# A decoder block on one core: ScalarE alone reads the transposed FFN input, the first weight group has its own buffer, and its preparation is interleaved with the residual adds

## The chip, the cores and the metric

One Trainium2 chip, one of its cores. The metric is the device time of one execution in microseconds. Three runs of the kernel before took 842.82, 843.07 and 843.86; their median is 843.07. One further execution was taken by the hardware profiler, and the profile and the trace are of that one.

The engines have these names here: PE does matmuls (PEld its weight loads), DVE is VectorE, ACT is ScalarE, POOL is GpSimd, and SP issues DMAs. Each works through its own queue in program order, and they meet through semaphores.

## The reference, cut to what matters

One decoder layer over 512 positions and 1024 channels in fp32. What bears on this change is the end of the first sub-layer and the start of the second:

```python
    x = x + gate1 * (merged @ w_out)
    h2 = rms_norm(x, norm2_g) * (1.0 + scale2) + shift2
    f_g, f_u = jnp.split(h2 @ w_ffn_in, 2, axis=-1)
    x = x + gate2 * ((jax.nn.silu(f_g) * f_u) @ w_ffn_out)
```

Ahead of it stand adaLN modulation, a combined input projection, a gated MLP over chunks and a sparse attention with an indexer; behind it stands a final RMSNorm. D_FF is 2816.

## The kernel before, in words

The kernel is one program with an order written out by hand: each engine executes in the order in which the Python code names its instructions. Each fp32 matrix product is made of three matmuls (`mm3`, L51 to L55): every operand is split into a high part, a copy rounded to the matmul type that ACT makes, and a low part, the remainder, that DVE (sometimes POOL) makes by a subtraction; the products high × high, high × low and low × high are added in PSUM. So each block of weights costs one ACT and one DVE instruction before PE may use it.

Weights come through a stream. `ensure(i)` issues the DMAs of the coming entries as long as one of the three rotating `raw` buffers can be promised (L92), and does the split of all entries up to `i` (`prep`: ACT at L112, the low part at L116). An entry can name fixed buffers (`where`) in place of the rotating `hi` and `lo`, and can have its low part put off (`"later"`), which then is done by calling `stream[i]["do"]()`.

The stretch around the change has these stages:

- **The output projection's last products** (loop from L1341). PSUM tiles `po`: for each half of the positions (two tiles of 128 rows) and each half h of the columns, two weight entries `W_O` give 24 matmuls of 512 columns. `resid` (L1152) then does, for each of the two row tiles, a DVE multiply by the gate (L1155), a DVE add into x (L1156) and an ACT square with a sum along the row (L1157). Meanwhile `ensure` splits the four entries `WF0` of the first FFN weights.
- **The norm of a half.** `row_rstd` (L1159) reduces the sums on DVE and takes the power on POOL. `norm2_x` (L1172) scales one row tile on DVE (L1179) and one on ACT (L1177).
- **The transposition.** `norm2_T(half)` (L1181) makes four PSUM banks `x2T` of four transposes each (PE, L1198). Each bank holds two blocks of 128x256. In the kernel before, DVE reads one block with scale and shift (L1208) and ACT the other (L1206); ACT makes the high part of both (L1210) and DVE the low part (L1213). `norm2_T(0)` stands amid the last products of the second half, `norm2_T(1)` amid the first FFN matmuls.
- **The first FFN columns** (`pf`, L1554 on): 192 matmuls of 256 columns, first for half 0, then for half 1. `t_diff` (L1410) and `t_split` (L305, L306) make from the blocks of both halves the four sums and differences that the next stage needs.
- **The seven-product groups** (loop over q from −2 to 17, tiles `R`). Each is a Strassen-like scheme of seven products on 2x2 blocks of a weight group. `s_issue(q)` (L1232) loads the two raw tiles of a group, `s_prep(q)` gives four pairs of an ACT split and DVE work on them (a0, d0 at L1257 to L1262; a1, d1 at L1266 to L1270; a2, d2 at L1274 and L1277; a3, d3 at L1281 and L1284). The work for group q+1 is put between the products of group q.

For the first group, q = −2, that work stands ahead of the loop: the raw tiles take two of the three rotating `raw` buffers and are issued after the first residuals; a0 and d0 stand behind `norm2_x(0)`; a2, d2, a1 and d1 behind `norm2_x(1)`; a3 and d3 amid the `t_split` calls of half 1. The order between residuals, norm and block work is:

```python
            for e in range(2):
                resid(po[e], 512 * h, 512, h, 2 * half + e, gate_b[1])
            if half == 0:
                ensure(WF0[2 + h])
                if h == 0:
                    s_issue(-2)
        if half == 0:
            for e in range(2):
                row_rstd(e)
            norm2_x(0)
            pre = s_prep(-2)
            for fn in pre[0]:
                fn()
```

Of the kernel before, what the change touches and what calls it, by code (L numbers as in the profile page):

```python
# [28 lines left out]
def block_kernel(ctx: ExitStack, tc: tile.TileContext, x, positions, w_ada, b_ada, w_in,  # L29
# [15 lines left out]
    def f(ap):  # L45
        return ap.bitcast(F32)
# [208 lines left out]
    for g in range(4):  # L255
# [903 lines left out]
    def row_rstd(tk):  # L1159
        V.tensor_reduce(r2[:, tk:tk + 1], ss2[:, tk], op=OP.add, axis=AX.X)  # L1160
        P.tensor_tensor(r2[:, tk:tk + 1], r2[:, tk:tk + 1], mhalf[:, :1], op=OP.pow)  # L1161


    HB = {}
    for kh in range(2):
        for th in range(2):
            HB[kh, th] = [base.tile([128, 4, 256], F32R, name="h2", tag=f"S2_{(kh * 2 + th) * 2 + e}", bufs=1)
                          for e in range(2)]
    h2f = {}
    xn = {}  # L1170

# [9 lines left out]
    def norm2_T(half, also={}):  # L1181
        if half == 0:
            for kh in range(2):
                t = ffn[0].tile([128, 4, 256], F32, name="h2f", tag=f"F{kh}", bufs=1)
                h2f["t", kh, 0] = [t[:, 0:2], t[:, 2:4]]
        else:
            for kh in range(2):
                h2f["t", kh, 1] = []
                for q in range(2):
                    t = base.tile([128, 2, 256], F32, name="h2f", tag=f"S1_{kh * 2 + q}", bufs=1)  # L1190
                    h2f["t", kh, 1].append(t)
        low = []
        for k2 in range(4):
            p = bank(4 + k2, "x2T")
            for k in range(2):
                kt = k2 * 2 + k
                for e in range(2):
                    T.transpose(p[:, k * 256 + e * 128:k * 256 + (e + 1) * 128],  # L1198
                                xn[2 * half + e][:, kt * 128:(kt + 1) * 128], ident)
            hf = h2f["t", k2 // 2, half][k2 % 2]  # L1200
            for k in range(2):
                kt = k2 * 2 + k
                g, s = Gc[:, 1, kt:kt + 1], Gc[:, 1, 8 + kt:9 + kt]
                src = p[:, k * 256:(k + 1) * 256]
                if k:
                    A.activation(hf[:, k], src, AF.Identity, scale=g, bias=s)  # L1206
                else:
                    V.tensor_scalar(hf[:, k], src, g, s, op0=OP.mult, op1=OP.add)  # L1208
            hi, lo = (t[:, 2 * (k2 % 2):2 * (k2 % 2) + 2] for t in HB[k2 // 2, half])
            A.activation(hi, hf, AF.Copy)  # L1210
            while low:
                low.pop()()
            low.append(lambda a=lo, b=hf, c=hi: V.tensor_sub(a, b, f(c)))  # L1213
            for fn in also.get(k2, ()):
                fn()
        low.pop()()


    NQ = 18
# [2 lines left out]
    def s_issue(q):  # L1222
        if q >= NQ:
            return
        c0 = (2 + q // 2) * 256 + (DFF if q % 2 else 0)
        sraw[q] = []
        for kh in range(2):
            if q % 2 and kh:
                t = ffn[0].tile([128, 4, 2, 128], F32, name="raw", tag="F0" if q > 0 else "E5", bufs=1)
            else:  # L1230
                t = base.tile([128, 4, 2, 128], F32, name="raw", tag="raw", bufs=RAWB)
            SY.dma_start(t.rearrange("p j a n -> p j (a n)"),  # L1232
                         w_ffn_in[kh * 512:(kh + 1) * 512, c0:c0 + 256].rearrange("(j p) n -> p j n", p=128))
            sraw[q].append(t)
# [10 lines left out]
    def s_prep(q):  # L1245

        if q >= NQ:
            return z_first()
        ra, rb = sraw[q]
        d = sw[q] = {}  # L1250
        A11, A21, A12, A22 = ra[:, :, 0], ra[:, :, 1], rb[:, :, 0], rb[:, :, 1]

        def a0():
            d["A"] = tuple(base.tile([128, 4, 128], F32R, name="sa", tag="acc", bufs=2) if q == -2 else
                           base.tile([128, 4, 128], F32R, name="sa", tag=f"S1_{4 + 2 * (q % 2) + e}", bufs=1)
                           for e in range(2))
            A.activation(d["A"][0], A11, AF.Copy)  # L1257

        def d0():
            V.tensor_add(A21, A21, A22)  # L1260
            V.tensor_sub(d["A"][1], A11, f(d["A"][0]))
# [23 lines left out]
        return [(a0, d0), (a1, d1), (a2, d2), (a3, d3)]  # L1285


    def seed(Z, ZB, dst, src):
# [49 lines left out]
    ffn.append(ctx.enter_context(tc.tile_pool(name="ffn", bufs=1)))  # L1338
    ensure(W_O[3])
    add_kept(O, 3, 2)  # L1340
    for half in range(2):  # L1341
        for h in range(2):
            po = O[2 * half + h]
            for n_, i in enumerate(W_O[2 * h:2 * h + 2]):
                hi, lo = chunk[i]
                for e in range(2):
                    opt_a_mm(po[e], 2 * half + e, hi, lo, stream[i]["kts"], mT, 8, False)
                if (half, h, n_) == (0, 0, 0):
                    ensure(WF0[1])
                if (half, h, n_) == (1, 1, 0):  # L1350
                    norm2_T(0)
            for e in range(2):
                resid(po[e], 512 * h, 512, h, 2 * half + e, gate_b[1])
            if half == 0:
                ensure(WF0[2 + h])
                if h == 0:
                    s_issue(-2)
        if half == 0:
# [12 lines left out]

    gate_b[2] = base.tile([128, D], F32, name="gate2b", tag="gate", bufs=1)
# [34 lines left out]

    TB = {}

    def t_diff():  # L1410
        for q in range(2):
# [144 lines left out]
    for half in range(2):  # L1556
        o = slice(half * 256, (half + 1) * 256)
        for w in range(2):
            for ci, i in enumerate(W_F[w]):
                hi, lo = chunk[i]  # L1560
                for j, kt in enumerate(stream[i]["kts"]):
                    for m in range(2):
                        cc = slice(m * 128, (m + 1) * 128)
                        mm3(pf[w][m][:, o], (hi[:, j, cc], lo[:, j, cc]), tuple(t[:, j] for t in HB[ci, half]),
                            kt + half == 0, kt == 7, skip_group_check=True)
                if half == 0 and w == 1 and ci == 0:
                    norm2_T(1)
            if half == 0 and w == 1:
                t_diff()
            if half == 1 and w == 0:  # L1570
                s_issue(-1)
            if half == 1:
                if w == 0:
                    EV[w](0)(pf[w])
                t_split(w + 1)
                if w == 1:
                    for fn in pre[3]:
                        fn()
                    t_split(3)
                    EV[w](0)(pf[w])  # L1580
                    t_split(4)
# [8 lines left out]
    for q in range(-2, NQ):  # L1590
# [30 lines left out]
        pre[0][0]()  # L1621
        sprod(R[0], d["A"], HB[0, 0], True)
        A.activation(R[1], R[0], AF.Copy)  # L1623
        pre[0][1]()
# [6 lines left out]
        pre[1][0]()  # L1631
        pre[1][1]()
        sprod(R[1], S2_, TB[2], False)
        A.activation(R[2], R[1], AF.Copy)
        pre[2][0]()
# [235 lines left out]
```

## Time and profile before

| what | us |
|---|---|
| median of three runs | 843.07 |
| lowest and highest of them | 842.82, 843.86 |
| the profiled execution, by the clock of the device | 842.46 |
| its span, first to last instruction | 840.7 |

Its mean granted TensorE clock is 0.995 of full speed. The busy shares of the engines follow below with the lines that the prediction rests on.

A timeline row gives the start in microseconds from the start of the span, the duration, engine and line, the operation with the tile that it writes and those that it reads, and in brackets the idle time of the engine before it and the instruction that ended it. A row of waits gives what waited for what, the total, the count and the longest. A row of groups gives the count, then busy time and mean duration in ns, then the idle time before. A window row gives for each engine its busy time and its count of instructions, then the granted clock of PE (1.00 is full speed), the share of the DMA engines and the GB/s. A matmul's duration is longer than the distance to the next one, since they are pipelined; what a matmul costs is the distance from start to start.

### The profile page before, as it was taken

Reading aid. Unit: us, or ns where it says so; the run is one execution under the profiler, and the core shown is the slowest. Engines: PE = TensorE matmul, PEld = TensorE weight load, DVE = VectorE, ACT = ScalarE, POOL = GpSimd, SP = SyncE. Lnnn points to the kernel's source line nnn. Section 1 sums busy time; section 2 is a strip of 40 time slices with the busy share of each in tenths; the row PEclk is TensorE's granted clock in tenths of the full one; section 3 lists DMA queues with packets and bytes.
Section 4 is the critical chain, followed back from the end, with each engine's and each line's share of the span. In section 5 each row is a group of like instructions: output and inputs, shape, how many; then the busy total and the mean of one; then the engine's idle time right before and its main releaser. Section 6 shows DMA issues by size and latency. Waiting matters only on the chain. (4 is left out here: it accounts for less than half of the span.)

```text
span 840.7 us, 12867 instructions
## 1 busy us (share of the span) xinstructions
PE 824.4 (98%) x4980; PEld 733.6 (87%) x4980; DVE 678.3 (81%) x1169; ACT 410.1 (49%) x714; POOL 108.3 (13%) x101
## 2 busy tenths in 40 slices
PE   7999999999999999999999989999999999999996
PEld 6888889988888888988888879999999999888885
DVE  7978799788899558887697779889998888985635
ACT  5664445322332226665536457555555555663322
POOL 2060022353344411000000000000000000000001
PEclk9999999999999999999999999999999999999998
DMA  9962362432346652047532402345543334143212
GB/s 297 308 193 71 96 200 77 127 89 86 106 147 199 190 172 90 26 154 228 196 100 62 139 26 76 109 157 163 167 158 102 102 101 147 54 141 104 82 50 101
DMA packets 95677, 109.10 MB, mean 130 GB/s; under 512 B 5616, under 2 KB 76272, under 8 KB 95616
## 3 DMA queue, kind: packets, MB, share of 16 engines
q1 hardware_dynamic: 92512, 101.37, 39.6%
q0 software_dynamic: 2384, 6.10, 2.1%
q8 instruction: 39, 0.64, 0.3%
q10 hardware_dynamic: 720, 0.82, 0.3%
q14 instruction: 22, 0.18, 0.1%
HBM read 105.90 MB, written 2.10 MB: 128 GB/s over the span
## 5 line engine op out<-in xcount | busy, mean ns | idle before, releaser
L112 ACT ACTIVATE hi<-raw 128x1024 fp32r<-128x1024 f32 (+2 forms) x82 | 84.6, 1034 | 106.2 <-PE pb L54 35.3
L116 DVE TENSOR_TENSOR lo<-raw,hi 128x1024 fp32r<-128x1024 f32 (+2 forms) x46 | 55.5, 1211 | 43.3 <-ACT hi L112 43.2
L116 POOL TENSOR_TENSOR lo<-raw,hi 128x1024 fp32r<-128x1024 f32 x29 | 73.3, 2529 | 128.5 <-ACT hi L112 122.8
L53 PE MATMUL pb<-h,hi 128*128 128x512 f32 x192 | 76.4, 398 | 0.0
L55 PE MATMUL pb<-h,lo 128*128 128x512 f32 x192 | 75.8, 395 | 0.0
L54 PE MATMUL pb<-hl,hi 128*128 128x512 f32 x192 | 75.8, 395 | 0.0
L177 DVE SCALAR_TENSOR_TENSOR acc<-mraw,cols,acc 128x512 f32<-128x512 f32 x49 | 39.8, 812 | 17.9 <-DMA mraw<-in_w_ada_dram 16.8
L55 PE MATMUL pfo<-hi,gs 128*128 128x512 f32 (+1 forms) x126 | 46.5, 369 | 0.0
L54 PE MATMUL pfo<-lo,gs 128*128 128x512 f32 (+1 forms) x126 | 46.4, 369 | 0.0
L53 PE MATMUL pfo<-hi,gs 128*128 128x512 f32 (+1 forms) x126 | 46.4, 368 | 0.0
L53 PE MATMUL R<-tb,sx 128*128 128x256 f32 x160 | 45.3, 283 | 0.5 <-ACT R L1623 0.5
L54 PE MATMUL R<-tb,sx 128*128 128x256 f32 x160 | 45.1, 282 | 0.0
L55 PE MATMUL R<-tb,sx 128*128 128x256 f32 x160 | 45.1, 282 | 0.0
L53 PE MATMUL R<-tb,hi 128*128 128x256 f32 x160 | 44.9, 281 | 0.0
L55 PE MATMUL R<-tb,lo 128*128 128x256 f32 x160 | 44.8, 280 | 0.0
L54 PE MATMUL R<-tb,hi 128*128 128x256 f32 x160 | 44.6, 279 | 0.0
L55 PEld LDWEIGHTS pb<-h,lo 128*128 128x128 f32 x192 | 36.0, 188 | 8.8
L54 PEld LDWEIGHTS pb<-hl,hi 128*128 128x128 f32 x192 | 36.0, 188 | 8.3
L53 PEld LDWEIGHTS pb<-h,hi 128*128 128x128 f32 x192 | 36.0, 188 | 8.3
L54 PE MATMUL pav<-lo,h 128*128 128x256 f32 x128 | 35.8, 280 | 0.0
L53 PE MATMUL pav<-hi,h 128*128 128x256 f32 x128 | 35.8, 279 | 0.0
L55 PE MATMUL pav<-hi,hl 128*128 128x256 f32 x128 | 35.8, 279 | 0.0
(400 smaller groups left out, 2660.7 us busy)
## 6 DMA issues: line engine op xcount, KB each, us to landing
raw<-in_w_ffn_in_dram SPq DMA_DIRECT2D x44, 512.0 KB, 4.3
raw<-in_w_in_dram SPq DMA_DIRECT2D x40, 512.0 KB, 3.9
mraw<-in_w_ada_dram SPq DMA_DIRECT2D x28, 512.0 KB, 4.1
raw<-in_w_ffn_out_dram SPq DMA_DIRECT2D x17, 512.0 KB, 3.9
s<-in_w_ada_dram SPq DMA_DIRECT2D x30, 256.0 KB, 5.5
raw<-in_w_proj_a_dram SPq DMA_DIRECT2D x8, 512.0 KB, 4.8
raw<-in_w_proj_b_dram SPq DMA_DIRECT2D x8, 512.0 KB, 4.7
raw<-in_w_in_dram SPq DMA_DIRECT2D x9, 256.0 KB, 4.7
```

Source lines behind the costliest of these rows:

```text
L53: T.matmul(o, wh, rh, start=start, stop=False, **kw)
L54: T.matmul(o, wh, rlo, start=False, stop=False, **kw)
L55: T.matmul(o, wlo, rh, start=False, stop=stop, **kw)
L112: A.activation(hi[:, :m], e["raw"][:, :m], AF.Copy)
L116: e["lo"].tensor_sub(lo[:, :m], e["raw"][:, :m], f(hi[:, :m]))
L177: V.scalar_tensor_tensor(o, w, cs[:, j:j + 1], o, op0=OP.mult, op1=OP.add)
```

## The change

1. **ACT alone reads the transposed banks.** In `norm2_T` both blocks of a bank are read by ACT; the DVE read goes. The low parts are not done in `norm2_T` any more: it returns them as a list, and the caller places them.
2. **A buffer of their own for the raw blocks of group −2.** They go to a tile `E2` of the `ffn` pool, which later holds the first `t_split` result, in place of two rotating `raw` buffers; `s_issue(-2)` moves ahead, behind `ensure(WF0[1])`.
3. **The block work of group −2 is interleaved with the residuals.** d0 and d1 are cut in two (d0a, d0b, d1a, d1b), and all of a0 to a3 and d0 to d3 are done by the end of the output projection. The low parts of the third and fourth FFN entries are put off and placed by hand. The reduces of half 0 come ahead of them.
4. **Other places for the weights of the output projection.** All four `W_O` entries have fixed buffers among `S2_0` to `S2_7`, those of column half 0 in the ones that half 0 of the FFN input takes afterwards, those of column half 1 in the ones for half 1. Accordingly the tiles `HB` are allocated in `norm2_T`.
5. **`t_diff` is called for one part at a time** in half 1, the first part ahead of the last low part.

```diff
-           ((0, 4, ("S2_2", "S2_3")), (0, 6, ("S2_6", "S2_7")), (1, 4, None), (1, 6, None))]
+           ((0, 4, ("S2_0", "S2_1")), (0, 6, ("S2_4", "S2_5")), (1, 4, ("S2_2", "S2_3")), (1, 6, ("S2_6", "S2_7")))]
...
-                if k:
-                    A.activation(hf[:, k], src, AF.Identity, scale=g, bias=s)
-                else:
-                    V.tensor_scalar(hf[:, k], src, g, s, op0=OP.mult, op1=OP.add)
+                A.activation(hf[:, k], p[:, k * 256:(k + 1) * 256], AF.Identity, scale=Gc[:, 1, kt:kt + 1],
+                             bias=Gc[:, 1, 8 + kt:9 + kt])
             hi, lo = (t[:, 2 * (k2 % 2):2 * (k2 % 2) + 2] for t in HB[k2 // 2, half])
             A.activation(hi, hf, AF.Copy)
-            while low:
-                low.pop()()
             low.append(lambda a=lo, b=hf, c=hi: V.tensor_sub(a, b, f(c)))
-            for fn in also.get(k2, ()):
-                fn()
-        low.pop()()
+        return low
...
+        both = ffn[0].tile([128, 2, 4, 2, 128], F32, name="raw", tag="E2", bufs=1) if q == -2 else None
         for kh in range(2):
-            if q % 2 and kh:
+            if both is not None:
+                t = both[:, kh]
+            elif q % 2 and kh:
...
-        def d0():
+        def d0a():
             V.tensor_add(A21, A21, A22)
+
+        def d0b():
             V.tensor_sub(d["A"][1], A11, f(d["A"][0]))
             V.tensor_sub(A11, A21, A11)
...
-        def d1():
+        def d1a():
             V.tensor_sub(d["B"][1], rb, f(d["B"][0]))
+
+        def d1b():
             V.tensor_sub(rb, rb, A11[:, :, None, :].to_broadcast([128, 4, 2, 128]))
...
+    for w in WF0[2:4]:
+        stream[w]["lo"] = "later"
...
                 if (half, h, n_) == (0, 0, 0):
                     ensure(WF0[1])
+                    s_issue(-2)
                 if (half, h, n_) == (1, 1, 0):
-                    norm2_T(0)
-            for e in range(2):
-                resid(po[e], 512 * h, 512, h, 2 * half + e, gate_b[1])
-            if half == 0:
-                ensure(WF0[2 + h])
-                if h == 0:
-                    s_issue(-2)
-        if half == 0:
-            for e in range(2):
-                row_rstd(e)
-            norm2_x(0)
-            pre = s_prep(-2)
-            for fn in pre[0]:
-                fn()
-    for e in range(2, 4):
-        row_rstd(e)
-    norm2_x(1)
-    for fn in pre[2] + pre[1]:
-        fn()
+                    low = norm2_T(0)
+            if (half, h) == (0, 0):
+                res(0)
+                ensure(WF0[2])
+                res(1)
+                stream[WF0[2]]["do"]()
+                (a0, d0a, d0b), (a1, d1a, d1b), (a2, d2), (a3, d3) = s_prep(-2)
+                a0()
+            elif (half, h) == (0, 1):
+                res(0)
+                res(1)
+                ensure(WF0[3])
+                d0a()
+                row_rstd(0)
+                row_rstd(1)
+                norm2_x(0)
+                d0b()
+                a2()
+            elif (half, h) == (1, 0):
+                res(0)
+                res(1)
+                stream[WF0[3]]["do"]()
+                d2()
+                a1()
+            else:
+                low[0]()
+                d1a()
+                low[1]()
+                res(0)
+                low[2]()
+                low[3]()
+                res(1)
+                row_rstd(2)
+                row_rstd(3)
+                norm2_x(1)
+                d1b()
+                a3()
+                d3()
...
                 if half == 0 and w == 1 and ci == 0:
-                    norm2_T(1)
-            if half == 0 and w == 1:
-                t_diff()
+                    low = norm2_T(1)
+                    for fn in low[:3]:
+                        fn()
+                    t_diff(0)
+                    low[3]()
+                    t_diff(1)
...
                 if w == 1:
-                    for fn in pre[3]:
-                        fn()
                     t_split(3)
```

More of the change, by code (lines that the diff above doesn't have):

```diff
@@ L1164, in block_kernel @@
     HB = {}
[L1165 to L1168, printed above, removed]
     h2f = {}
@@ L1179, in norm2_x, with norm2_T @@
                 V.tensor_scalar(xn[tk], xt[tk], r2[:, tk:tk + 1], None, op0=OP.mult)
-    def norm2_T(half, also={}):
-        if half == 0:
-            for kh in range(2):
+    def norm2_T(half):
+        for kh in range(2):
+            HB[kh, half] = [base.tile([128, 4, 256], F32R, name="h2", tag=f"S2_{(kh * 2 + half) * 2 + e}", bufs=1)
+                            for e in range(2)]
+            if half == 0:
                 t = ffn[0].tile([128, 4, 256], F32, name="h2f", tag=f"F{kh}", bufs=1)
                 h2f["t", kh, 0] = [t[:, 0:2], t[:, 2:4]]
-        else:
[L1187 to L1191, printed above, removed]
+            else:
+                h2f["t", kh, 1] = [base.tile([128, 2, 256], F32, name="h2f", tag=f"S1_{kh * 2 + q}", bufs=1)
+                                   for q in range(2)]
         low = []
@@ L1284, in d3 @@
             V.tensor_sub(d["D"][1], rb, f(d["D"][0]))
-        return [(a0, d0), (a1, d1), (a2, d2), (a3, d3)]
+        return [(a0, d0a, d0b), (a1, d1a, d1b), (a2, d2), (a3, d3)]
     def seed(Z, ZB, dst, src):
@@ L1343, in block_kernel, with res @@
             po = O[2 * half + h]
+            def res(e):
+                resid(po[e], 512 * h, 512, h, 2 * half + e, gate_b[1])
             for n_, i in enumerate(W_O[2 * h:2 * h + 2]):
@@ L1408, in block_kernel, with t_diff @@
     TB = {}
-    def t_diff():
-        for q in range(2):
+    def t_diff(*qs):
+        for q in qs:
             b11, b21, b12, b22 = (h2f["t", kh, th][q] for th in range(2) for kh in range(2))
@@ L1623, in block_kernel @@
         A.activation(R[1], R[0], AF.Copy)
-        pre[0][1]()
+        for fn in pre[0][1:]:
+            fn()
         while left:
@@ L1630, in block_kernel @@
         A.activation(ps[0], R[3], AF.Copy)
-        pre[1][0]()
-        pre[1][1]()
+        for fn in pre[1]:
+            fn()
         sprod(R[1], S2_, TB[2], False)
```

5 lines of the change are left out of this document (1 added, 4 removed).

## The prediction

> **What bounds the kernel now.** I read the page first, then the waits of PE, then PE's own instructions in order of time.
>
> ```profile
> span 840.7 us, 12867 instructions
> PE 824.4 (98%) x4980; PEld 733.6 (87%) x4980; DVE 678.3 (81%) x1169; ACT 410.1 (49%) x714; POOL 108.3 (13%) x101
> raw<-in_w_ffn_in_dram SPq DMA_DIRECT2D x44, 512.0 KB, 4.3
> PE pf L53 <- ACT h L1210: 2.8, 2, 1.9
> ```
>
> PE is busy 98% of the span, so only what makes PE stand still or run slowly can give time. The row of waits (total, times, longest) ends on the transposed input of the FFN: its first matmuls (pf) wait for the high part of the block (ACT, L1210) and, in the next fence, for its low part (DVE, L1213). That is the place that the change touches. The next fence is PE in order of time around it: start, duration, line, and in brackets the idle time before.
>
> ```profile
> 484.55 0.39 PE L54 MATMUL po<-lo,mt 128*128 128x512 f32 x1
> 484.78 0.40 PE L55 MATMUL po<-hi,mt 128*128 128x512 f32 x1
> 487.09 0.39 PE L53 MATMUL pf<-h,wx 128*128 128x256 f32 x1 [1.91 <-ACT h L1210]
> 487.81 0.39 PE L54 MATMUL pf<-h,wx 128*128 128x256 f32 x1 [0.34 <-DVE h L1213]
> ...
> 491.56 0.30 PE L54 MATMUL pf<-h,wx 128*128 128x256 f32 x1
> ...
> 497.87 1.91 PE L1198 MATMUL x2T<-cst,xn 128*128 128x128 f32 x16
> 499.54 0.36 PE L53 MATMUL pf<-h,wx 128*128 128x256 f32 x1
> ...
> 502.35 0.28 PE L55 MATMUL pf<-h,wx 128*128 128x256 f32 x1
> 503.54 0.38 PE L53 MATMUL pf<-h,wx 128*128 128x256 f32 x1 [0.92 <-ACT h L1210]
> 504.26 0.39 PE L54 MATMUL pf<-h,wx 128*128 128x256 f32 x1 [0.34 <-DVE h L1213]
> ...
> 515.61 0.28 PE L53 MATMUL R<-h,sa 128*128 128x256 f32 x1
> ...
> 528.37 0.28 PE L55 MATMUL R<-tb,sx 128*128 128x256 f32 x1
> 529.11 0.39 PE L53 MATMUL R<-tb,sx 128*128 128x256 f32 x1 [0.46 <-ACT R L1623]
> ```
>
> And the same stretch in windows (PE busy and its count first, then the other engines, then the granted clock):
>
> ```profile
> 487.90:491.56 3.66, 3.66 (x19) 3.66 (x20) 3.06 (x6) 2.53 (x5) 0.00 (x0) 0.53 0.00 0
> 491.56:497.87 6.31, 6.31 (x54) 6.31 (x54) 3.23 (x7) 3.30 (x6) 2.07 (x3) 1.00 0.09 32
> ```
>
> At full clock a 256-column matmul comes every 6.31/53 = 0.119 us (54 in the window, the last one overlapping). The 512-column ones come every 0.23 (484.55 to 484.78). So the last po matmul's slot ends at 485.01. The losses of the stretch:
> - first half: 487.09 − 485.01 = 2.08, then 0.72 − 0.12 = 0.60 for the low part;
> - right behind it the granted clock is 0.53 to 491.56: 18 matmuls from 487.81 take 3.75 instead of 18 × 0.119 = 2.14, a loss of 1.61;
> - second half: 503.54 − 502.35 − 0.12 = 1.07, and 504.26 − 503.54 − 0.12 = 0.60;
> - later, 529.11 − 528.37 − 0.12 = 0.62.
>
> That is 6.58 us, 5.96 of them ahead of the seven-product groups (first R at 515.61). Check: 192 pf matmuls × 0.119 = 22.85 and 1.67 for 16 transposes (497.87 to 499.54) make 24.52 from 485.01, so 509.53 without a stall; 515.61 is 6.08 later. The skeleton closes to 0.1 us.
>
> Why are the blocks late? The chain ahead of them, on ACT and DVE:
>
> ```profile
> 475.45 1.04 ACT L112 ACTIVATE wx<-raw 128x1024 fp32r<-128x1024 f32 x1
> 479.34 1.15 ACT L1177 ACTIVATE xn<-xr,sm 128x1024 f32<-128x1024 f32 x1 [2.85 <-POOL sm L1161]
> 480.40 0.61 ACT L1257 ACTIVATE sa<-raw 128x512 fp32r<-128x512 f32 x1
> 483.87 0.63 ACT L1157 ACTIVATE rt<-xr 128x512 f32<-128x512 f32 x1 [2.86 <-issue]
> 484.41 0.19 ACT L1157 ACTIVATION_READ_ACCUMULATOR rt<-xr 128x1 f32 x1
> ...
> 485.83 0.55 ACT L1206 ACTIVATE h2f<-x2T,Gc 128x256 f32<-128x256 f32 x1
> 486.40 0.63 ACT L1210 ACTIVATE h<-h2f 128x512 fp32r<-128x512 f32 x1
> 486.94 0.55 ACT L1206 ACTIVATE h2f<-x2T,Gc 128x256 f32<-128x256 f32 x1
> ```
> ```profile
> 466.36 0.68 DVE L1155 TENSOR_TENSOR rt<-po,gate1b 128x512 f32<-128x512 f32 x1
> ...
> 476.52 1.23 DVE L116 TENSOR_TENSOR wx<-raw,wx 128x1024 fp32r<-128x1024 f32 x1 [1.80 <-ACT wx L112]
> ...
> 481.04 0.69 DVE L1261 TENSOR_TENSOR sa<-raw,sa 128x512 fp32r<-128x512 f32 x1 [1.18 <-ACT sa L1257]
> ...
> 482.38 0.68 DVE L1155 TENSOR_TENSOR rt<-po,gate1b 128x512 f32<-128x512 f32 x1
> ```
>
> DVE waits 1.80 for ACT's split of an FFN weight before it may reduce the row sums; POOL's power and ACT's scaling of xn come behind that; DVE then waits 1.18 for the first block split; so the residuals of the second half start at 482.38 although their matmuls were due at 477.8 (485.01 less 24 × 0.23 and 1.67 of transposes). Their squares hold ACT to 485.83, and only there it begins on the blocks. The blocks are late by program order; neither engine is full.
>
> **The change part by part.** Durations: square with its accumulator read 0.73 (483.87 to 484.60), split of 1024 columns 1.04 on ACT and 1.23 on DVE, of 512 columns 0.61 and 0.69, xn 1.15 on ACT. Dependent instructions follow after about 0.02, independent ones overlap by about 0.1. Three more rows, of groups and of POOL, and a pair of ACT reads of one transposed bank, which is what a block of ACT alone looks like:
>
> ```profile
> L1206 ACT ACTIVATE h2f<-x2T,Gc 128x256 f32<-128x256 f32 x8 | 4.4, 554 | 3.4 <-DVE h2f L1208 3.2
> L1208 DVE TENSOR_SCALAR h2f<-x2T,Gc 128x256 f32<-128x256 f32 x8 | 4.1, 536 | 0.0
> 494.99 0.99 POOL L1161 TENSOR_TENSOR sm<-sm,mhalf 128x1 f32<-128x1 f32 x1 [0.33 <-DVE sm L1160]
> 36.81 0.78 ACT L434 ACTIVATE h<-xT,G 128x512 fp32r<-128x512 f32 x1
> 37.49 0.77 ACT L436 ACTIVATE hf<-xT,G 128x512 f32<-128x512 f32 x1
> ```
>
> *ACT alone.* Per half four DVE reads (4 × 0.54) go and four ACT reads come. The pair at L434/L436 shows that the second read starts 0.10 before the first ends, so a bank costs ACT 0.46 + 0.57 (read, then the dependent hi) + 0.54 = 1.57 where the shared way had 1.11 from one read to the next (485.83 to 486.94). This slows the four highs of a half by up to 1.8; bounds for a bank are 1.57 and 1.9 (two reads at the 0.68 of the wider pair). I take 1.57, the nearer width.
>
> The Trainium skill, TensorEngine Tiling (Array Packing), section PSUM Bottleneck, says to use both ScalarE and VectorE for evacuation, which speaks against this part. The rows agree on one bank (1.11 against 1.57); by that rule alone the sum would be up to 1.8 per half worse, and the time lost only where PE has no spare.
>
> *First half, interleaved.* Counting on from 466.36 with the new order. DVE: two residuals with the 1.23 split of the third FFN weight behind them, to 470.7; the two of the second product 471.0 to 473.8; the add of block work (d0a) 474.4; reduces as soon as the squares are in, 474.75; POOL to 475.9; ACT's xn to 477.1, where the transposes are due only at 480.6 (485.01 less 12 × 0.23 and 1.67): 3.5 spare. The reduce no longer stands behind the fourth weight's split. DVE: xn, two block subtractions to 477.0, residuals 476.9 to 479.6, the fourth weight's low part 480.75, block low part 481.9. ACT: block split 478.1, squares to 480.4, block split 481.35, then the banks: highs at 482.9, 484.5, 486.05, 487.6. Low parts with d1a and a residual between: 483.6, 485.4, 487.3, 488.3. PE wants them at 485.15, 486.6, 488.0, 489.4 (6 matmuls × 2 × 0.119 = 1.43 per bank): spare 1.5, 1.2, 0.7, 1.1. So 2.08 + 0.60 go.
>
> *Second half.* Last residual 489.6, square 490.4, reduce, POOL 0.99, xn at 492.8; PE reaches the transposes at 485.01 + 72 × 0.119 = 493.6: spare 0.8. ACT's last block split to 493.7, highs at 495.7, 497.3, 498.9, 500.4. Low parts 496.45, 498.0, 499.6; then four t_diff subtractions (0.70 each, as L1213) stand ahead of the last low part: 502.9. PE wants them at 498.2, 499.7, 501.1 and 502.5. The last is late: a stall of 0.4 where there were 1.07 + 0.60. What is queued behind it on DVE is t_diff and t_split, done at 512.6 where the first R product starts at 510.0.
>
> *The clock.* With no idle of 2 us the slow stretch should go too: it stood only behind the idle of 1.91 + 0.34, and 0.92 + 0.34 at 503.54 left the clock at 1.0 (the matmuls behind 504.26 keep 0.119). I take 1.61 as gained; the bounds are 0 and 1.61.
>
> The Trainium skill, TensorE: Matmul & The Clock Gate, Part 1, gives an idle window of about 3.4 us before the clock is halved. The row differs: 2.3 us of idle within 2.8 sufficed here. Read strictly, by that rule the slow stretch had another cause and stays.
>
> *Blocks in a buffer of their own.* Two DMAs of 512 KB move ahead on SP, past the third weight's wait, and no longer need slots of the rotating raw buffer.
>
> ```profile
> 465.17 0.37 SPq L92 DMA_DIRECT2D raw<-in_w_ffn_in_dram  x1
> ...
> 472.09 0.37 SPq L1232 DMA_DIRECT2D raw<-in_w_ffn_in_dram  x1
> GB/s 0 0 75 328 358 166 183 258 266 295 377 265 99 167 375 273 10 143 299 372 176 229 277 200 53 0 0 0 46 220 340 249 17 22 7 0 0 0 123 309
> ```
>
> In the kernel before the second one goes out at 472.09; in the new order both stand right behind 465.17. The last line is the rate in slices of 0.6 us from 456: the ten slices from 464.4 average 235 GB/s, so 1.57 MB land by about 472. First use on ACT 470.2, behind the second residual's square, and on DVE 473.7. Bounds: 470.3 (4.3 after issue) and 478.1 (three lone landings of 4.3 in a row); with the second bound all that follows would be 4 later. I take 472: no cost.
>
> *Third gap.* 529.11 waits for an ACT copy queued behind activations that wait for DVE:
>
> ```profile
> 527.07 0.42 DVE L1646 TENSOR_TENSOR fs<-R,ps 128x256 f32<-128x256 f32 x1
> ```
>
> That is 11.5 after the first R product. DVE is then 4.8 behind PE; afterwards 2.6 (512.6 − 510.0), with one 1.23 split already done: 9.7 after. The 0.62 goes.
>
> *Weights of w_out in other buffers.* Same splits, and the places are free; nothing is added.
>
> **Sum.** 2.08 + 0.60 + 1.61 + 1.67 + 0.62 − 0.4 = 6.2. The profiled execution took 842.46 (span 840.7 and 1.76 around it): 836.3. The median of the three runs, 843.07, is 0.61 above it: 836.9; with 0.1 for small waits 837.0.
>
> **The rivals.**
> - *ACT becomes the bound of the blocks.* At 1.9 a bank the highs of each half come 1.3 later; the first half's spare takes half of that, the second has none, and the last stall grows from 0.4 to about 2.2: 838.8. For: 12 instructions in a row on one engine. Against: ACT is busy 49%. Chance 0.14.
> - *The slow stretch stays.* Then 1.61 is not gained: 838.6. For: it is one event. Against: it begins with the stall. Chance 0.08. By the Trainium skill's rule above the time would come out so.
> - *Slower: the blocks land late.* a0 stands in ACT's queue, and d0a in DVE's, ahead of the row sums and residuals. If the new buffer is freed late (it lies over memory of the stage before, and no row shows when that is released), each microsecond after 474.1 costs one. The gain is gone at a landing of 480.3 and 0.2% is lost from 482.0; a landing at 485.0 gives 843.07 + 10.9 − 6.2 = 847.8. For: SP waits are long here already. Against: in the code all readers of that memory come before the last stage of w_out's products. Chance 0.10.
> - *It doesn't do what it says:* PE's first wait falls but another of the same length takes its place (low parts behind residuals on DVE), 842.5. Against: 0.7 to 1.5 spare. Chance 0.06.
>
> **How the numbers follow.** The forecast has 0.62, 835.3 (all stalls gone and some gained behind) to 838.4; with the first two rivals 0.84, up to 840.0 if both come together in part. So the range is 835.3 to 840.0. A measurement here tells about 0.2%, 1.7 us, from no change. Faster: 0.62 + 0.14 + 0.08 = 0.84; same 0.06; slower 0.10.
>
> **What would show it.** Right: no PE wait over 0.5 us for L1210's successor in the first half, no window at 0.53 clock there, a wait under 1 us for the last low part of the second half, the first R product near 510, nothing before 529's counterpart. Wrong: ACT or DVE waiting for a DMA of raw near 470 to 474; transposes waiting for xn; slow clock again; hi to hi well over 1.6.

## The result and the profile after

The changed kernel takes 836.41 us (median of 4 runs, 836.07 to 836.56), the kernel before 842.95 beside it; the ratio is 0.992, with a 95% interval of 0.9903 to 0.9937. It is faster by 6.5 us, under 1% of the time. The profiled execution of the changed kernel took 836.07, its span is 834.3, so 6.4 less than the span before.

The waits of PE are the first thing to read. These are all that the view lists for the changed kernel (total, times, longest):

```profile
PE warm L442 <- DMA cst<-in_consts_dram: 4.8, 1, 4.8
PE pf L54 <- DVE h L1203: 0.5, 1, 0.5
PE modS L415 <- DVE accw L177: 0.4, 1, 0.4
```

The first and the third lie in the first 20 us and were there before. Of the waits for the transposed input one is left, for a low part (L1203 is L1213 of the kernel before), and the wait of the first groups for an ACT copy is gone. PE in order of time, as before (start, duration, line, in brackets the idle time before):

```profile
460.89 0.39 PE L53 MATMUL po<-wx,mt 128*128 128x512 f32 x1
...
484.50 0.39 PE L55 MATMUL po<-wx,mt 128*128 128x512 f32 x1
484.73 0.28 PE L53 MATMUL pf<-h,wx 128*128 128x256 f32 x1
484.85 0.28 PE L54 MATMUL pf<-h,wx 128*128 128x256 f32 x1
...
493.31 1.91 PE L1194 MATMUL x2T<-cst,xn 128*128 128x128 f32 x16
...
502.17 0.28 PE L53 MATMUL pf<-h,wx 128*128 128x256 f32 x1
502.95 0.39 PE L54 MATMUL pf<-h,wx 128*128 128x256 f32 x1 [0.50 <-DVE h L1203]
...
510.03 0.28 PE L53 MATMUL R<-h,sa 128*128 128x256 f32 x1
```

The last `po` matmul and the first `pf` matmul now stand 0.23 apart, with no idle time; before there were 2.31. From 484.73 to 502.17 there is nothing but full-clock spacing, and the windows say the same (PE busy and count first, the granted clock third from the end):

```profile
484.73:488.40 3.67, 3.67 (x32) 3.66 (x31) 3.27 (x7) 3.53 (x8) 0.00 (x0) 1.00 0.00 0
488.40:493.31 4.91, 4.91 (x43) 4.91 (x42) 3.34 (x7) 2.22 (x4) 2.06 (x3) 1.00 0.01 3
```

The stretch at 0.53 clock is gone. The chain that feeds PE, first ACT, then DVE, of the changed kernel:

```profile
469.99 0.63 ACT L1248 ACTIVATE sa<-raw 128x512 fp32r<-128x512 f32 x1 [0.32 <-DMA raw<-in_w_ffn_in_dram]
...
475.75 1.16 ACT L1173 ACTIVATE xn<-xr,sm 128x1024 f32<-128x1024 f32 x1 [0.42 <-POOL sm L1161]
...
481.32 1.00 ACT L1199 ACTIVATE h2f<-x2T,Gc 128x256 f32<-128x256 f32 x2
482.35 0.63 ACT L1202 ACTIVATE h<-h2f 128x512 fp32r<-128x512 f32 x1
482.89 1.01 ACT L1199 ACTIVATE h2f<-x2T,Gc 128x256 f32<-128x256 f32 x2
...
498.15 0.63 ACT L1202 ACTIVATE h<-h2f 128x512 fp32r<-128x512 f32 x1
...
499.73 0.63 ACT L1202 ACTIVATE h<-h2f 128x512 fp32r<-128x512 f32 x1
```
```profile
473.47 0.68 DVE L1251 TENSOR_TENSOR raw<-raw 128x512 f32<-128x512 f32 x1
...
483.02 0.69 DVE L1203 TENSOR_TENSOR h<-h2f,h 128x512 fp32r<-128x512 f32 x1 [1.09 <-ACT h L1202]
...
486.69 0.68 DVE L1203 TENSOR_TENSOR h<-h2f,h 128x512 fp32r<-128x512 f32 x1
...
498.82 0.69 DVE L1203 TENSOR_TENSOR h<-h2f,h 128x512 fp32r<-128x512 f32 x1 [0.88 <-ACT h L1202]
499.43 0.68 DVE L1434 TENSOR_TENSOR h2f<-h2f 128x512 f32<-128x512 f32 x1
...
502.21 0.69 DVE L1203 TENSOR_TENSOR h<-h2f,h 128x512 fp32r<-128x512 f32 x1
```

ACT's reads begin at 481.32 instead of 485.83: 4.5 earlier, or 4.2 when both are counted from the first `po<-wx` matmul below. A bank costs ACT 1.57 (481.32 to 482.89). The last wait of PE is read off DVE: the fourth high ends at 500.36, but its low part starts only at 502.21, behind four differences from 499.43 on.

**Where the 6.4 come from.** As a ruler I take two starts that every kernel has: the first matmul of the last products (`po<-wx`) and the first matmul of the seven-product groups (`R<-h,sa`).

| part of the span | before | after | difference |
|---|---|---|---|
| start to first `po<-wx` | 461.23 | 460.89 | 0.34 |
| to first `R<-h,sa` (the stretch) | 54.38 | 49.14 | 5.24 |
| to the end | 325.09 | 324.27 | 0.82 |

The first row is not the change's: in the runs below this start lies anywhere between 460.89 and 462.17. The stretch is steadier: two profiles of one kernel agree in it within 0.05. Where two versions differ by less than a microsecond, their run times overlap, and the comparison rests on the stretches of their profiles.

### The profile page after: what moved, and what is told of

Its sections match the earlier page's. It is cut to its first block, busy times and chain, and to the rows that moved or that the text cites. A ratio compares the mean times of both kernels' runs of the same rounds, so it can differ in the third digit from the quotient of the medians.

```text
span 834.3 us, 12856 instructions
## 1 busy us (share of the span) xinstructions
PE 821.6 (98%) x4980; PEld 731.2 (88%) x4980; DVE 674.6 (81%) x1161; ACT 414.1 (50%) x722; POOL 108.1 (13%) x101
## 4 chain that ended last, share of the span: by engine, by line
PE 95%; DMA 1%; DVE 1%; ACT 1%; issue 0%; SPq 0%; POOLq 0%; POOL 0%; DVEq 0%
PE pb L53 9%; PE pb L55 9%; PE pb L54 9%; PE R L53 8%; PE R L54 8%; PE R L55 8%; PE pfo L55 5%; PE pfo L54 5%; PE pfo L53 4%; PE pav L54 2%; PE pav L53 2%; PE pav L55 2%; PE pgb L53 2%; PE pgb L54 2%; PE pgb L55 2%; PE po L54 2%
## 5 line engine op out<-in xcount | busy, mean ns | idle before, releaser
L112 ACT ACTIVATE hi<-raw 128x1024 fp32r<-128x1024 f32 (+2 forms) x80 | 82.5, 1034 | 104.1 <-PE pb L54 43.7
L116 DVE TENSOR_TENSOR lo<-raw,hi 128x1024 fp32r<-128x1024 f32 (+2 forms) x44 | 53.0, 1211 | 41.9 <-ACT hi L112 41.7
```

The source lines that it names most:

```text
L112: A.activation(hi[:, :m], e["raw"][:, :m], AF.Copy)
L116: e["lo"].tensor_sub(lo[:, :m], e["raw"][:, :m], f(hi[:, :m]))
```

## The experiments

All stretches below are R start less `po<-wx` start of the run's own trace; 49.14 and 836.41 are the changed kernel's.

**1. DVE reads one block of each bank again,** all else as changed.

```diff
-                A.activation(hf[:, k], p[:, k * 256:(k + 1) * 256], AF.Identity, scale=Gc[:, 1, kt:kt + 1],
-                             bias=Gc[:, 1, 8 + kt:9 + kt])
+                g, s = Gc[:, 1, kt:kt + 1], Gc[:, 1, 8 + kt:9 + kt]
+                src = p[:, k * 256:(k + 1) * 256]
+                if k:
+                    A.activation(hf[:, k], src, AF.Identity, scale=g, bias=s)
+                else:
+                    V.tensor_scalar(hf[:, k], src, g, s, op0=OP.mult, op1=OP.add)
```

> The changed kernel, but DVE again reads the first block of each transposed bank and ACT the second. Theory (the gain is the interleaving; ACT alone is worth next to nothing in the new order): 836.4 to 837.2, with the first matmul of the seven-product groups within 0.8 us of 510.0; the four DVE reads push the first low part from 483.0 to about 483.8 and PE stands for some 0.3 us more in each half. Rival (ACT alone carries the gain of the second half, 1.7 us, because it takes the reads off a loaded DVE): 838 or more.

837.04 us (836.87 to 837.34), ratio to the kernel before 0.9934 (0.9921 to 0.9946). Stretch 511.03 − 461.34 = 49.69, 0.55 more. The DVE row of this run shows what ACT alone avoids, four reads in front of the first low part:

```profile
482.30 1.89 DVE L1204 TENSOR_SCALAR h2f<-x2T,Gc 128x256 f32<-128x256 f32 x4
484.13 0.69 DVE L1207 TENSOR_TENSOR h<-h2f,h 128x512 fp32r<-128x512 f32 x1
```
```profile
488.54 0.39 PE L54 MATMUL pf<-h,wx 128*128 128x256 f32 x1 [0.21 <-DVE h L1207]
503.94 0.39 PE L54 MATMUL pf<-h,wx 128*128 128x256 f32 x1 [0.57 <-DVE h L1207]
```

So in the new order ACT alone is worth about half a microsecond: 0.47 of the 0.55 at the low part of 488.54, in the first half, and only 0.08 in the second, where 0.3 in each half was foretold. The theory's range of times holds the run, and the rival (1.7) is out; the first `R` matmul lies 1.0 from 510.0, not within 0.8, as `po<-wx` too starts 0.45 later in this run. The intervals of the two ratios overlap, so the 0.55 rests on the profiles.

**2. ACT alone in the old order:** the kernel before with the reverse of the edit above.

> The kernel before with one edit: ACT alone reads the transposed banks. Theory (worth next to nothing by itself): 842.5 to 843.4; in the first half the highs come 0.46 later each, the first PE wait grows from 1.91 to about 2.4 and the slow clock stays; in the second half the waits of 0.92 and 0.34 shrink, because ACT no longer waits for a DVE that is busy with block work, but transposes and last low parts take up what that gives. Rival 1 (evacuation by one engine is the bound): slower by 2 us or more, 845. Rival 2 (it frees the second half): faster by 1.7 us, 841.3.

842.64 us (841.72 to 843.52, 11 runs), ratio 1.0002 (0.9993 to 1.001): no difference. Both rivals (845 and 841.3) are out. PE's waits moved mostly as the theory has it, and the half clock behind the first of them stayed (last row):

```profile
487.52 0.39 PE L53 MATMUL pf<-h,wx 128*128 128x256 f32 x1 [2.29 <-ACT h L1206]
488.25 0.58 PE L54 MATMUL pf<-h,wx 128*128 128x256 f32 x1 [0.34 <-DVE h L1209]
498.82 1.86 PE L1198 MATMUL x2T<-cst,xn 128*128 128x128 f32 x15 [0.30 <-ACT xn L1177]
504.02 0.39 PE L54 MATMUL pf<-h,wx 128*128 128x256 f32 x1 [0.39 <-DVE h L1209]
```
```profile
488.50:491.40 2.90, 2.90 (x14) 2.90 (x15) 1.39 (x2) 2.87 (x6) 0.00 (x0) 0.50 0.00 0
```

The first wait grew by 0.38, the one of 0.92 for a high in the second half is gone, the one of 0.34 for its low part is 0.39 and did not shrink, and a new one for xn came. Stretch 515.37 − 461.34 = 54.03, 0.35 less than before: too little for the run times.

**3. The raw blocks in the rotating buffers again.**

```diff
-        both = ffn[0].tile([128, 2, 4, 2, 128], F32, name="raw", tag="E2", bufs=1) if q == -2 else None
+        both = ffn[0].tile([128, 2, 4, 2, 128], F32, name="raw", tag="E2", bufs=1) if q == -3 else None
...
                     ensure(WF0[1])
-                    s_issue(-2)
...
                 stream[WF0[2]]["do"]()
+                s_issue(-2)
```

No group has the number −3, so every raw block goes to the rotating buffers.

> The changed kernel, but the raw blocks of group -2 go to the rotating buffers again, issued as early as these allow. Theory (the buffer is there so that the second raw block lands in time): it can go out only when the third FFN weight's low part is made, at 470.3, lands near 474.4, and d0a at the head of DVE's chain starts 1 us later than 473.5; the first half's spare takes part of it, PE loses 0.5 to 1 us: 836.9 to 837.5. Rival (the buffer is worth nothing, all spare): 836.4, within 0.2.

836.65 us (836.16 to 837.18), ratio 0.9929 (0.9916 to 0.9941). Stretch 510.91 − 461.30 = 49.61, 0.47 more. The median lies 0.24 above the changed kernel's, within what the runs scatter and below the theory's range, so the times decide nothing between theory and rival; the trace shows the wait that was foretold:

```profile
474.51 0.69 DVE L1251 TENSOR_TENSOR raw<-raw 128x512 f32<-128x512 f32 x1 [0.55 <-DMA raw<-in_w_ffn_in_dram]
```

The block work's first DVE step waits for the second raw block. Counted from `po<-wx` it starts at 13.21 instead of 12.58, so 0.63 later, and PE loses 0.47 of that.

**4. The four low parts ahead of the eight differences.**

```diff
-                    for fn in low[:3]:
+                    for fn in low:
                         fn()
-                    t_diff(0)
-                    low[3]()
-                    t_diff(1)
+                    t_diff(0, 1)
```

> The changed kernel, but in the second half all four low parts come before the eight differences. Theory (the last PE wait of 0.50, a loss of 0.66 from start to start, comes from the four differences ahead of the last low part): that wait goes, the first seven-product matmul is 0.6 to 0.7 earlier against the first FFN matmul, the sums on DVE end 0.9 later but still ahead of their use: 835.6 to 835.9. Rival (the wait moves to the sums or to the first groups): 836.4, and a new wait of PE behind 510.

835.94 us (835.54 to 836.79), ratio 0.9921 (0.9908 to 0.9935). The profile has no PE wait in the stretch at all; 510.43 − 462.05 = 48.38, 0.76 less, and the rest to the end is unchanged (834.7 − 510.43 = 324.27). As the run times scatter by more than that, it was run again beside the changed kernel.

> The changed kernel once more, as the yardstick for the next run on the same chip. Theory: 49.1 us from the first matmul of the last products to the first seven-product matmul, ratio to the kernel before 0.992 to 0.993.

> The kernel with all four low parts ahead of the differences, once more beside the changed kernel. Theory (the differences ahead of the last low part cost 0.7): stretch 48.4, median 0.6 to 0.8 below that of the changed kernel, no PE wait in the stretch. Rival (given back behind): medians within 0.2.

The changed kernel: 836.34 us (836.18 to 837.29), ratio 0.9927 (0.9914 to 0.9939), stretch 510.16 − 460.97 = 49.19. With the low parts first: 835.42 us (834.99 to 835.9), ratio 0.9913 (0.9899 to 0.9926), stretch 509.89 − 461.51 = 48.38 again. No run of the one lies within the runs of the other; the medians are 0.9 apart, the stretches 0.8. This version is faster than both kernels, by 0.8 in the profiles against the changed one, and 48.38 is what the stretch takes if PE never waits: 96 products of 0.23, 192 of 0.119 and two times 1.67 for transposes make 48.3.

**5. The block work back at its old places,** with reduces, residuals and low parts as changed.

```diff
-                a0()
...
                 ensure(WF0[3])
-                d0a()
...
                 norm2_x(0)
+                a0()
+                d0a()
                 d0b()
-                a2()
...
                 stream[WF0[3]]["do"]()
-                d2()
-                a1()
...
                 low[0]()
-                d1a()
...
                 norm2_x(1)
+                a2()
+                d2()
+                a1()
+                d1a()
                 d1b()
-                a3()
-                d3()
...
+                if w == 0:
+                    a3()
+                    d3()
                 t_split(w + 1)
```

> The changed kernel, but the block work of group -2 goes back to where the kernel before had it: a0 and d0 behind the first half's xn, a2, d2, a1, d1 behind the second half's xn, a3 and d3 ahead of the first sum split. Reduces, residuals and deferred low parts stay as changed. Theory (the early reduce saves the first half, the interleaved blocks save the second): no PE wait over 0.5 us in the first half and no slow clock, but in the second half a1 and d1 stand ahead of the highs and low parts, so the waits there grow to about 2.3 in all, and some 0.3 of the wait in the first groups returns: 838.2 to 839.2. Rival 1 (where the block work stands is worth nothing): 836.4. Rival 2 (it is worth nearly all): 841 or more, with the slow clock back.

838.64 us (838.02 to 839.19), ratio 0.9949 (0.9936 to 0.9961). Stretch 512.95 − 462.17 = 50.78, 1.64 more, and 0.18 more behind it. All PE waits of the stretch, and the DVE work that makes them:

```profile
489.39 0.38 PE L54 MATMUL pf<-h,wx 128*128 128x256 f32 x1 [0.23 <-DVE h L1203]
500.34 0.39 PE L54 MATMUL pf<-h,wx 128*128 128x256 f32 x1 [0.38 <-DVE h L1203]
505.86 0.39 PE L54 MATMUL pf<-h,wx 128*128 128x256 f32 x1 [1.00 <-DVE h L1203]
```
```profile
496.06 1.23 DVE L1272 TENSOR_TENSOR lo<-raw,hi 128x1024 fp32r<-128x1024 f32 x1 [2.57 <-ACT hi L1269]
497.20 1.22 DVE L1262 TENSOR_TENSOR lo<-raw,hi 128x1024 fp32r<-128x1024 f32 x1
498.46 1.23 DVE L1265 TENSOR_TENSOR raw<-raw 128x1024 f32<-128x1024 f32 x1
499.60 1.28 DVE L1203 TENSOR_TENSOR h<-h2f,h 128x512 fp32r<-128x512 f32 x2
```

Three block operations of 1.2 us stand ahead of the second half's low parts. The first half stays nearly whole and at full clock. The time is in the theory's range, but the waits of the second half, foretold at about 2.3, are 1.4 in the view. So, with the rest as changed, the interleaving of the blocks gives about 1.8 of the 6.5.

**6. The fourth weight's low part ahead of the row sums again.**

```diff
                 ensure(WF0[3])
+                stream[WF0[3]]["do"]()
                 d0a()
...
                 res(1)
-                stream[WF0[3]]["do"]()
                 d2()
```

> The changed kernel, but the fourth FFN weight's low part stands ahead of the first half's row sums again, as in the kernel before. Theory (chain of squares, xn, blocks and residuals): everything on DVE behind it comes 3 us later, the first high lands near 486.1, PE waits about 1.2 for it and 0.35 for its low part, and more of the 3 us is paid at later low parts: 838.5 to 839.5; with an idle of 1.2 + 0.35 the clock stays at 1.0. Rival (xn has 3.5 us of spare ahead of the transposes, so it costs nothing): 836.6. Rival on the clock: this idle already brings a stretch near 0.53.

839.86 us (839.03 to 840.71), ratio 0.9964 (0.9951 to 0.9976). Stretch 514.65 − 461.96 = 52.69, 3.55 more: the largest of all single steps, for moving one instruction of 1.23 us. DVE, PE and a window of this run:

```profile
476.43 1.23 DVE L114 TENSOR_TENSOR wx<-raw,wx 128x1024 fp32r<-128x1024 f32 x1 [1.80 <-ACT wx L112]
477.57 0.68 DVE L1251 TENSOR_TENSOR raw<-raw 128x512 f32<-128x512 f32 x1
```
```profile
487.13 0.39 PE L53 MATMUL pf<-h,wx 128*128 128x256 f32 x1 [1.16 <-ACT h L1202]
487.86 0.38 PE L54 MATMUL pf<-h,wx 128*128 128x256 f32 x1 [0.34 <-DVE h L1203]
```
```profile
488.40:491.60 3.20, 3.20 (x17) 3.20 (x16) 3.03 (x5) 3.14 (x7) 0.00 (x0) 0.50 0.00 0
```

The instruction waits 1.80 for its ACT split, as in the kernel before, and all that is queued on DVE waits with it: the row sums, xn, the blocks, the residuals, and through their squares ACT. It is slower than the theory's range because of the third fence: an idle of 1.16 + 0.34 was enough for half the clock. The theory on the clock was wrong here, its rival right. Of the 3.55, the two waits make 2.04 from start to start, 0.1 for the restart behind them included; the 1.5 that are left are the matmuls at half clock.

**7. Two superfluous ACT splits in the changed kernel.**

```diff
                 a1()
+                for _ in range(2):
+                    A.activation(sw[-2]["B"][0], sraw[-2][1], AF.Copy)
```

> The changed kernel, with the ACT split a1 done three times instead of once (two superfluous instructions of 0.95 us each, just ahead of the first half's reads; the result is the same). Theory (in the changed kernel the chain from the first highs over residual, square, xn, second highs and four differences to the last low part has no spare, so a delay costs its length): 838.2, plus 1.7 to 2.0 on the stretch. Rival (the first half has 0.7 to 1.5 us of spare, as the prediction had it, and takes it up): plus 0.4 to 1.2, 836.8 to 837.6.

838.83 us (838.12 to 839.29), ratio 0.995 (0.9938 to 0.9963). Stretch 512.80 − 461.64 = 51.16, 2.02 more. The two added instructions took 2.15 together; PE paid nearly all of it. The same two in the kernel with the low parts first:

> The kernel with the low parts first, with two superfluous ACT splits (1.9 us) ahead of the first half's reads. In the changed kernel the same two cost 2.0 on the stretch. Theory (that chain had no spare only because of the differences ahead of the last low part): the three PE waits of the first half stay, 0.32, 0.34 and 0.23 (1.3 from start to start), the wait of the second half is gone, stretch 49.6 to 49.9, which is 1.2 to 1.5 more than without the splits. Rival (a delay costs its length in any case): 2.0 more, 50.4.

837.71 us (837.36 to 838.54), ratio 0.994 (0.9928 to 0.9953). Stretch 511.36 − 460.99 = 50.37, 1.99 more than 48.38: the rival's number, not mine. The second half has no wait, as I expected, but the first half's waits are not 1.3 in all:

```profile
485.32 0.39 PE L53 MATMUL pf<-h,wx 128*128 128x256 f32 x1 [0.32 <-ACT h L1202]
486.05 0.39 PE L54 MATMUL pf<-h,wx 128*128 128x256 f32 x1 [0.34 <-DVE h L1203]
...
487.45 0.28 PE L53 MATMUL pf<-h,wx 128*128 128x256 f32 x1
487.79 0.39 PE L54 MATMUL pf<-h,wx 128*128 128x256 f32 x1
...
489.72 0.39 PE L54 MATMUL pf<-h,wx 128*128 128x256 f32 x1 [0.23 <-DVE h L1203]
```

From start to start they cost 0.49, 0.61 and 0.40, the second low part (487.45 to 487.79) 0.22 more that the view doesn't list as a wait, and each of three restarts 0.1. My theory that only the differences take the spare away falls: the first half alone has only 0.36 at its third low part.

**8. Four and three superfluous splits with the low parts first,** to make PE wait as long as before and somewhat less.

> The kernel with all four low parts ahead of the differences, with a1 done five times (four superfluous instructions, 3.8 us, ahead of the first half's reads; the result is the same). PE then waits about 2.0 for the first high and 0.35 for its low part, as in the kernel before. Theory (an idle of about 2 + 0.35 us brings the slow clock): a stretch with a clock near 0.55 of some 3.5 us behind the wait, and 4.0 to 4.4 more than the kernel without the added splits, 839.9 to 840.3. Rival (the slow clock of the kernel before had another cause): full clock, and 3.1 to 3.5 more, 839.0 to 839.4.

> The same with three superfluous splits (2.85 us): PE waits about 1.27 for the first high and 0.34 for its low part, beside 1.16 and 0.34 in the run with the late reduce, whose clock went slow, and 0.92 and 0.34 in the second half of the kernel before, whose clock did not. Theory (an idle of about 1.2 and more brings the slow clock): a stretch near 0.5 of some 3.4 us, stretch 51.9 to 52.3. Rival (length alone doesn't decide, the moment does): full clock in this run, stretch 50.7 to 51.1.

Four: 840.43 us (840.24 to 841.42), ratio 0.9976 (0.9966 to 0.9986), stretch 514.21 − 460.96 = 53.25, 4.87 more. Three: 839.6 us (838.7 to 839.88), ratio 0.9958 (0.9944 to 0.9971), stretch 513.56 − 462.10 = 51.46, 3.08 more. First the run with four, its two waits and a window behind them, then the same of the run with three (its first two waits):

```profile
487.48 0.38 PE L53 MATMUL pf<-h,wx 128*128 128x256 f32 x1 [2.50 <-ACT h L1202]
488.20 0.39 PE L54 MATMUL pf<-h,wx 128*128 128x256 f32 x1 [0.34 <-DVE h L1203]
```
```profile
489.20:492.40 3.20, 3.20 (x17) 3.20 (x17) 2.80 (x6) 3.14 (x7) 0.00 (x0) 0.50 0.00 0
```
```profile
487.52 0.38 PE L53 MATMUL pf<-h,wx 128*128 128x256 f32 x1 [1.41 <-ACT h L1202]
488.25 0.39 PE L54 MATMUL pf<-h,wx 128*128 128x256 f32 x1 [0.34 <-DVE h L1203]
```
```profile
488.40:491.60 3.20, 3.16 (x24) 2.84 (x24) 3.17 (x5) 3.12 (x7) 0.00 (x0) 1.00 0.00 0
```

Seventeen matmuls against twenty-four in 3.2 us. With four splits the slow clock is back, so the rival falls, but both time and stretch lie above the theory's range. The splits take 2.15, 3.24 and 4.33 on ACT for two, three and four; two and three cost the stretch 0.16 less than that (1.99 and 3.08), four 0.54 more (4.87). So I estimate that the slow clock costs some 0.7 net here. PE runs slower behind the wait, but with two and with three splits it waits again at the second and third low part, and with four it no longer does.

With three, an idle of 1.41 + 0.34 left the clock at 1.0, though 1.16 + 0.34 had halved it in run 6; the idle was longer than the foretold 1.27, so the stretch fits neither range, and on the clock the rival is right. So the long idle brings the slow clock, and near 1.5 us length alone does not decide. The mean granted clocks of the five executions with three splits point the same way: 0.998 (the profiled one), 0.999 and 0.999, but 0.995 twice, while no run of the other versions whose profile has no slow stretch lists less than 0.997. Of one and the same kernel, two executions seem to have had the slow stretch and three not; only the profiled one has a trace.

## Why the prediction was right, point by point

The time was foretold at 837.0 with a range of 835.3 to 840.0; 836.41 lies 0.6 below the forecast. Step by step:

- **First half, 2.08 + 0.60 gone: right.** The path was as described: reduces at once, xn at 475.75 (foretold end 477.1, measured 476.91), ACT's reads from 481.32, first low part 483.02 (foretold to end at 483.6, measured 483.71); counted from `po<-wx` the two came 0.15 and 0.45 later than worked out, within the spare. Runs 5 and 6 show what carried it: the order of one low part against the row sums (3.55 of the stretch, the slow clock included), not the blocks. The spare was too large in the prediction at the third low part: 0.7 foretold; it ended at 487.37 and PE took it at 487.73, so 0.36. Run 7 shows that this makes a delay cost nearly its whole length.
- **The clock, 1.61: right in size,** and its rival (the slow stretch stays) is out: run 8 brought it back by idle time alone. The 1.61 is right as an entry in the account of the trace: without any wait the stretch takes 48.38 (run 4), and the kernel before lost 6.00 in it where the working has 5.96. It is not shown to be what the clock is worth by itself. In run 8 the estimate is 0.7. In run 2 six of eleven executions list a mean clock of 0.999, where 3.4 us at half clock would take 0.002 off the mean of 840 us, so these six seem to have gone without; they took 841.72 to 843.39, the other five 842.39 to 843.52. The reason given for it was too simple: it took 0.92 + 0.34 as short enough and 2.3 as long enough, and the runs put 1.16 + 0.34 on the slow side and 1.41 + 0.34 on the other.
- **Second half, 1.67 less a new stall of 0.4: right in kind, the stall mis-sized.** It measures 0.66, and 0.1 for the restart. Counted from `po<-wx`, the last low part ends at 42.01 (502.90) where the working had 41.67, and PE wants it at 41.40 where the working had 41.27: the chain of added durations came out 0.3 too short.
- **ACT alone, priced as up to 1.8 lost on the highs of a half and taken up by spare: the price of a bank is right** (1.57, measured 1.57), the sign of its effect is not: undone in the new order it costs 0.55, since DVE is the engine with work in front of the low parts. In the old order it was worth nothing that the times can tell. The Trainium skill, TensorEngine Tiling (Array Packing), section PSUM Bottleneck, would use both engines; here that is the slower form, by 0.55.
- **Own buffer, no cost: right,** and it gives 0.47 of stretch, which the prediction did not count. The slower rival's mechanism is real on a small scale: ACT's first split waited 0.32 for the DMA in the changed kernel, and in run 3 DVE waited 0.55 and PE lost 0.47. It needed a landing at 482 to win.
- **Third gap, 0.62: right;** the part behind the first R start is 0.82 shorter, the rest being two slots of 0.1 in the same group.

Sum of the terms: foretold 6.2, measured 5.24 + 0.82 = 6.06 on the two rows that belong to the change. That the two agree within 0.2 is partly luck: the new stall is 0.36 larger than foretold (0.76 with its restart), and the part behind the first R start gave 0.2 more. The forecast also took 0.61 from the profiled execution to the median of the runs and 0.1 for small waits; 0.34 was measured from the one to the other. The single steps undone (0.55, 0.47, 1.64, 3.55) are not terms of that sum; they were not tried in every combination. No run undoes the other places of the w_out weights; that they cost nothing rests on the account above closing without them.

## What to carry to other kernels

When PE waits for a short chain over several in-order engines, look for the instruction that stands ahead of the chain on its engine and itself waits for another engine: moving one low part of 1.23 us behind the row sums was worth 3.55 us, some 1.5 of it because the slow clock went with the wait; the transfer of the reads from DVE to ACT was worth 0.55. After such a change the chain may have next to no spare even where PE shows no wait at all; a few superfluous instructions in it measure the spare directly. And where a list is handed over in order, put what PE waits for ahead of what it will want later: that gave another 0.8.

## What the runs showed of the hardware

A stretch at half clock followed an idle of 1.91 + 0.34, 2.29 + 0.34, 2.50 + 0.34 and 1.16 + 0.34 us, and did not follow 1.41 + 0.34, 0.92 + 0.34 or 0.32 + 0.34; each pair is from one profiled execution. The Trainium skill, TensorE: Matmul & The Clock Gate, Part 1, tells of a free-running window of about 3.4 us and of a re-throttle after at least one idle window. The idle needed here is far shorter than that, so on this point the measurement decides; that the moment counts beside the length would fit a window that runs freely, and so would the two kinds of executions of the version with three splits (run 8), but no run here moved the same idle against such a window, and it stays open.

A matmul that resumes after such a wait costs about 0.1 us more until the next one (0.22 between the starts where 0.12 is usual), also at full clock; and where PE waits for a high part, it waits 0.34 again at the low part right behind.
